# Memory attention of a decoder layer: TensorE's instructions in the order of emission

## The chip, the cores and the metric

The kernel runs on one core of a Trainium2 chip. The time is that of the device for one execution of the whole program, in microseconds (us), as the median over runs. The core has five engines that run side by side, each with its own queue of instructions: TensorE (PE, with its weight loads as PEld), VectorE (DVE), ScalarE (ACT), GpSimd (POOL) and SyncE (SP), which here issues the DMA transfers.

## The reference

The program computes one decoder layer for 1024 tokens with d_model 1024: a half-step SwiGLU, then three branches from one projection (A: chunked spatial gating, B: causal latent attention, C: cross-attention into 256 memory tokens), their gated merge, an output projection and a second half-step SwiGLU. All inputs are float32. What this case touches is branch C, and the product of branch A with its weights that runs in between:

```python
def memory_attention(q_m, mem, mem_norm, w_kv, q_norm, k_norm):
    q = rmsnorm(q_m.reshape(B, S, MEM_HEADS, MEM_HEAD_DIM), q_norm)      # 4 heads of 128
    kv = rmsnorm(mem, mem_norm) @ w_kv
    k = rmsnorm(kv[..., :MEM_WIDTH].reshape(B, M, MEM_HEADS, MEM_HEAD_DIM), k_norm)
    v = kv[..., MEM_WIDTH:].reshape(B, M, MEM_HEADS, MEM_HEAD_DIM)       # M = 256
    s = jnp.einsum('bshd,bmhd->bhsm', q, k).astype(jnp.float32) * (MEM_HEAD_DIM ** -0.5)
    p = jax.nn.softmax(s, axis=-1)
    return jnp.einsum('bhsm,bmhd->bshd', p.astype(v.dtype), v).reshape(B, S, MEM_WIDTH)
...
merged = (gates[:, :, 0] * (y_a @ w_branch_a[l])      # the product that fills in
          + gates[:, :, 1] * (y_b @ w_branch_b[l])
          + gates[:, :, 2] * (y_c @ w_branch_c[l]))
```

## The kernel before

**Number format.** To keep float32 accuracy on TensorE, every operand is split in a rounded part and a rest (hi and lo, type fp32r). `split` does it: ScalarE copies to hi (L139), VectorE subtracts to lo (L142). A product is then three matmuls, `mm3`: hi by hi (L158), hi by lo (L159), lo by hi (L160).

**The stage.** `mem_attention` (L857) comes after the spatial gating and ahead of the causal attention. It works on eight tiles of 128 queries, numbered (i, k) with i = 0..3 and k = 0..1; two tiles make a pair i. It is a list of calls of small functions, written out by hand, with these letters:

- `S` (`scores`, L862): four heads, each one `mm3` of 256 columns, into one PSUM tile `mm` (two buffers): 12 matmuls. Then VectorE takes the extreme of each row (L874) and scales it (L878), ScalarE takes four exponentials (L882), VectorE the reciprocals of the sums (L886), GpSimd multiplies (L887).
- `T` (`turn`, L890): the eight transposes of a tile's probabilities (L934), in two calls of `to_feature4`, each four transposes into one PSUM tile `bank` and one `split`. "The eight turns of each tile" are these. `T` raises the priority of what it emits.
- `V` (`value`, L901): the product of a pair's probabilities with the values: 24 matmuls of 256 columns into two `bank` tiles, each split at once.
- `F` (a step of `branches`, L527): 12 matmuls of 512 columns of branch A's product into one `bank` tile, which VectorE multiplies with the gate (L1117) and SyncE stores. There are 16 such steps, called blocks here. `A` is such a step too, with an order for its casts on ScalarE.
- `Q` (`mem_queries`, L850): eight DMA loads (L855), of 256 KB each, of one half (512 tokens) of the queries: hi and lo of four heads. The tiles of heads 0 and 1 are called `h`, those of heads 2 and 3 `v_hi` and `v_lo`, after the buffers that they live in.
- `R`: a rotation on GpSimd that belongs to the next stage.

There are four `bank` buffers in all, for blocks, turns and values together.

**What sets the order.** The framework has a scheduler: before the program is built, it lays the instructions of each engine in one fixed order, by their priority (which falls in the order of emission, and which `T` raises) and by when, in its own model of time, their operands are there. The order on an engine at run time is that fixed order; an engine waits at an instruction whose operands are late, and nothing behind it passes. Parts of the program stand in a region (`manual_schedule`) in which named engines keep the order of emission instead. `mem_attention` stands in none before the change, so that the matmuls of blocks, scores, turns and values are mixed by the scheduler. SyncE's queue, too, is laid out by the scheduler.

Of the kernel before, what the change touches and what calls it, by code (L numbers as in the profile page):

```python
# [18 lines left out]
S = 1024  # L19
DT = D // P  # L20
NT = S // P
F = 2816
# [27 lines left out]
class Kernel:  # L50
# [806 lines left out]
    def mem_attention(self, qt, rooms, kt, vv, filler, after, aside):  # L857

        nc = self.nc
        r, nr = self.mq_r, self.mq_nr  # L860
        st, scaled = {}, []

        def scores(i, k):
            t = 2 * i + k
            sc = self.mm().rearrange("p a (b m) -> p (a b) m", b=2)
            for hh in range(MH):
                last = self.last
                first = self.mm3(
                    sc[:, hh], tuple(x[:, t * P:(t + 1) * P] for x in qt[hh]), tuple(x[:, hh] for x in kt),
                    True, True)  # L870
                if i == hh == 0:
                    self.after(first, last)
            mx = self.stat("m_mx", MH)
            m = nc.vector.tensor_reduce(mx, sc, axis=AXX, op=ALU.min)  # L874
            if scaled:
                self.after(m, scaled.pop())
            with self.tc.high_priority(offset=600):
                scaled.append(nc.vector.tensor_tensor(mx, mx, r[:, t], op=ALU.mult))  # L878
            pr = rooms[t % len(rooms)]
            sm = self.stat("m_sm", MH)  # L880
            for hh in range(MH):
                nc.scalar.activation(  # L882
                    pr[:, hh], sc[:, hh], ACT.Exp, bias=mx[:, hh:hh + 1], scale=nr[:, t, hh:hh + 1],
                    accum_out=sm[:, hh:hh + 1])
            rs = self.stat("m_rs", MH)
            nc.vector.reciprocal(rs, sm)  # L886
            nc.gpsimd.tensor_tensor(pr, pr, rs.unsqueeze(2).to_broadcast([P, MH, ML]), op=ALU.mult)  # L887
            st[i, k] = pr

        def turn(i, k):  # L890
            if k == 0:
                st[i] = [tuple(self.wide(n).rearrange("p (h q) -> p h q", h=MH) for n in ("whi", "wlo")) for _ in range(2)]
            pr = st.pop((i, k))
            for m in range(2):
                with self.tc.high_priority(offset=600):
                    self.to_feature4(
                        tuple(t[:, :, k * P:(k + 1) * P] for t in st[i][m]),
                        [pr[:, hh, m * P:(m + 1) * P] for hh in range(MH)])

        def value(i):  # L900
            pt = st.pop(i)  # L901
            for pair in range(MH // 2):
                o = self.bank().rearrange("p (b q) -> p b q", b=2)
                for hh in (2 * pair, 2 * pair + 1):
                    for m in range(2):
                        s = tuple(t[:, m, hh * MD:(hh + 1) * MD] for t in vv)
                        self.mm3(o[:, hh % 2], s, tuple(t[:, hh] for t in pt[m]), m == 0, m == 1)
                for hh in (2 * pair, 2 * pair + 1):
                    self.split(*(t[:, 2 * i * P:2 * (i + 1) * P] for t in yt[hh]), o[:, hh % 2])

        S, T, V = scores, turn, value
        R = lambda: aside(behind=self.last)
        F = lambda: next(filler, None)
        Q = lambda half: self.mem_queries(qt, half, self.sig_mark)

        def A():
            self.hold = after
            F()
            self.hold = None

        yt = [self.split_pair(self.h4) for _ in range(MH)]
        for f, *x in (
                (A,), (A,), (Q, 0), (S, 0, 0), (A,), (S, 0, 1), (F,), (F,), (Q, 1), (T, 0, 0), (S, 1, 0), (F,), (T, 0, 1), (S, 1, 1),
                (F,), (F,), (V, 0), (T, 1, 0), (S, 2, 0), (F,), (T, 1, 1), (S, 2, 1), (F,), (V, 1), (F,), (T, 2, 0),
                (S, 3, 0), (F,), (T, 2, 1), (S, 3, 1), (R,), (F,), (V, 2), (F,), (T, 3, 0), (F,), (T, 3, 1), (F,), (V, 3)):
            f(*x)
        for _ in filler:
            pass
        return yt
# [1402 lines left out]
```

## Time and profile before

| what | value |
|---|---|
| time, median of 3 runs | 2164.04 us (2162.85 to 2164.99) |
| the profiled execution | 2163.03 us, of which 2161.3 us are the span of the profile |
| granted TensorE clock, mean | 0.999 of full speed |
| busy share of the span: PE, DVE, ACT, POOL | 100%, 73%, 42%, 12% |
| the stage from its first block to its last value matmul | 1134.46 to 1209.18 us of the span |

In the rows of a timeline the first number is the start of a group of like instructions in us from the start of the span, the second how long the group took, and the text in brackets the idle time of the engine ahead of it with what ended it. Matmuls are pipelined: one ends after the next has begun, so that the pace of TensorE is read from one start to the next, not from the length of one.

### The profile page before, as it was taken

The page shows a single profiled execution, that of the slowest core. Times are in us where ns is not written, and L with a number is a line of the kernel's source. Part 1 is how long each engine was busy: PE and PEld are TensorE (multiplying, and loading weights), DVE is VectorE, ACT ScalarE, POOL GpSimd, SP SyncE. Part 2 cuts the span into 40 slices and gives each one's busy share as a digit, 9 for nine tenths or more (in the row PEclk, how much of TensorE's full clock was granted, in tenths as well). Part 3 has the DMA queues.
Part 4 walks back from the last instruction along what each step waited for, and adds up shares of the span by engine and source line. Part 5 has one row for each costly group of instructions (what it writes and reads, how often), then busy time and mean ns, then how long its engine had stood idle before and what let it go on. Part 6 is the DMA issues. An engine that isn't in the chain of part 4 may idle for free.

```text
span 2161.3 us, 27448 instructions
## 1 busy us (share of the span) xinstructions
PE 2151.9 (100%) x10112; PEld 1797.8 (83%) x10112; DVE 1572.1 (73%) x2371; ACT 910.3 (42%) x1486; POOL 255.0 (12%) x256
## 2 busy tenths in 40 slices
PE   9999999999999999999999999999999999999999
PEld 6888888888887888888988889988888888888887
DVE  7966666679889657655786679886876666657884
ACT  6433333243455434433555378833433223224332
POOL 0011111100000000000123311240011212110000
PEclk9999999999999999999999999999999999999999
DMA  4264555385332445641587832293133332347443
GB/s 148 92 220 159 190 180 175 119 318 193 118 124 94 147 164 180 223 149 61 212 283 259 314 105 69 75 348 104 40 127 103 110 97 100 103 144 288 169 129 104
DMA packets 137175, 342.56 MB, mean 158 GB/s; under 512 B 21713, under 2 KB 30033, under 8 KB 137041
## 3 DMA queue, kind: packets, MB, share of 16 engines
q1 hardware_dynamic: 136896, 340.81, 45.9%
q8 instruction: 79, 1.29, 0.2%
q14 instruction: 56, 0.45, 0.1%
q10 hardware_dynamic: 144, 0.00, 0.0%
HBM read 230.90 MB, written 109.86 MB: 158 GB/s over the span
## 4 chain that ended last, share of the span: by engine, by line
PE 91%; DVE 6%; ACT 1%; DMA 1%; issue 1%; SPq 0%; POOL 0%; ACTq 0%; DVEq 0%; POOLq 0%
PE one L158 15%; PE one L159 15%; PE one L160 15%; PE bank L158 13%; PE bank L159 13%; PE bank L160 13%; PE mm L158 1%; PE mm L159 1%; PE mm L160 1%; PE bank L1019 1%; PE one L1967 1%; DVE w L147 1%; DVE wlo L147 1%; DVE pr L997 1%; DVE wlo L142 1%
## 5 line engine op out<-in xcount | busy, mean ns | idle before, releaser
L146 ACT CAST whi<-x 128x1024 fp32r<-128x1024 f32 x202 | 192.3, 955 | 414.4 <-DVE x L1443 170.4
L147 DVE TENSOR_TENSOR wlo<-x,whi 128x1024 fp32r<-128x1024 f32 x202 | 241.2, 1195 | 58.9 <-ACT whi L146 19.6
L1471 DVE TENSOR_TENSOR t<-t,one 128x512 f32<-128x512 f32 x188 | 128.9, 686 | 190.8 <-PE one L160 190.7
L158 PE MATMUL bank<-h,whi 128*128 128x512 f32 x636 | 247.9, 390 | 0.0
L160 PE MATMUL bank<-h,wlo 128*128 128x512 f32 x636 | 247.5, 389 | 0.0
L159 PE MATMUL bank<-h,whi 128*128 128x512 f32 x636 | 247.5, 389 | 0.0
L158 PE MATMUL one<-h,whi 128*128 128x512 f32 x508 | 199.0, 392 | 0.0
L159 PE MATMUL one<-h,whi 128*128 128x512 f32 x508 | 198.4, 390 | 0.0
L160 PE MATMUL one<-h,wlo 128*128 128x512 f32 x508 | 198.3, 390 | 0.0
L158 PE MATMUL one<-w,whi 128*128 128x512 f32 x432 | 168.5, 390 | 0.0
L159 PE MATMUL one<-w,whi 128*128 128x512 f32 x432 | 168.1, 389 | 0.0
L160 PE MATMUL one<-w,wlo 128*128 128x512 f32 x432 | 168.1, 389 | 0.0
L142 DVE TENSOR_TENSOR wlo<-w,whi 128x1024 fp32r<-128x1024 f32 (+2 forms) x112 | 114.4, 1036 | 67.3 <-ACT whi L139 67.1
L139 ACT CAST whi<-w 128x1024 fp32r<-128x1024 f32 (+2 forms) x112 | 98.8, 901 | 149.8 <-PE one L159 55.6
L2067 POOL TENSOR_TENSOR raw<-raw 128x512 f32<-128x512 f32 x38 | 57.0, 1499 | 794.8 <-DVE raw L1908 684.8
L160 PEld LDWEIGHTS bank<-h,wlo 128*128 128x128 f32 x636 | 119.4, 188 | 24.9
L159 PEld LDWEIGHTS bank<-h,whi 128*128 128x128 f32 x636 | 119.4, 188 | 24.6
L158 PEld LDWEIGHTS bank<-h,whi 128*128 128x128 f32 x636 | 119.4, 188 | 24.4
L158 PE MATMUL bank<-whi 128*128 128x512 f32 x352 | 136.9, 389 | 0.0
L159 PE MATMUL bank<-wlo,whi 128*128 128x512 f32 x352 | 136.9, 389 | 0.0
L160 PE MATMUL bank<-whi,wlo 128*128 128x512 f32 x352 | 136.9, 389 | 0.0
L160 PEld LDWEIGHTS one<-h,wlo 128*128 128x128 f32 x508 | 95.8, 189 | 20.1
(406 smaller groups left out, 4892.2 us busy)
## 6 DMA issues: line engine op xcount, KB each, us to landing
x<-in_ffn_w_gu_dram SPq DMA_DIRECT2D x78, 512.0 KB, 5.1
w<-tdt SPq DMA_DIRECT2D x40, 512.0 KB, 4.2
gate<-raw SPq DMA_DIRECT2D x33, 512.0 KB, 3.0
tdb<-raw SPq DMA_DIRECT2D x64, 256.0 KB, 2.1
h<-in_ffn_w_down_dram SPq DMA_DIRECT2D x64, 256.0 KB, 6.0
w<-tdb SPq DMA_DIRECT2D x30, 512.0 KB, 5.1
tdt<-w SPq DMA_DIRECT2D x48, 256.0 KB, 2.4
x<-in_w_gate_dram SPq DMA_DIRECT2D x22, 512.0 KB, 5.9
```

The costliest lines, as they stand in the source:

```text
L139: i = self.nc.scalar.copy(hi, src)
L142: return (eng or self.nc.vector).tensor_tensor(lo, src, hi.bitcast(F32), op=ALU.subtract)
L146: self.nc.scalar.copy(hi, src)
L147: return lambda: self.nc.vector.tensor_tensor(lo, src, hi.bitcast(F32), op=ALU.subtract)
L158: i = mmul(out, s[0], m[0], start=first, stop=False, **kw)
L159: mmul(out, s[0], m[1], start=False, stop=False, **kw)
L160: self.last = mmul(out, s[1], m[0], start=False, stop=last, **kw)
L997: nc.vector.tensor_tensor_reduce(out=pr[:, :m], in0=sc[:, :m], in1=self.mask[:, m0:m0 + m], scale=1.0, scalar=-NEG, op0=ALU.add, op1=ALU.m ...
L1019: nc.tensor.transpose(b[:, at:at + P], prs[t][:, kk * P:(kk + 1) * P], self.ident)
L1471: return self.nc.vector.tensor_tensor(out, x, y, op=ALU.add)
L1967: k.last = nc.tensor.matmul(b, w, norm.x(half, c), start=c == 0, stop=c == DT - 1)
L2067: sub = lambda d, x, y: (eng or nc.gpsimd).tensor_tensor(d, x, y, op=ALU.subtract)
```

## The change

The list of calls is put into a region in which TensorE keeps the order of emission. The list itself, the arithmetic, the buffers and the other engines' instructions are as before; the order of the other engines stays with the scheduler.

```diff
         yt = [self.split_pair(self.h4) for _ in range(MH)]
-        for f, *x in (
-                (A,), (A,), (Q, 0), (S, 0, 0), (A,), (S, 0, 1), (F,), (F,), (Q, 1), (T, 0, 0), (S, 1, 0), (F,), (T, 0, 1), (S, 1, 1),
-                (F,), (F,), (V, 0), (T, 1, 0), (S, 2, 0), (F,), (T, 1, 1), (S, 2, 1), (F,), (V, 1), (F,), (T, 2, 0),
-                (S, 3, 0), (F,), (T, 2, 1), (S, 3, 1), (R,), (F,), (V, 2), (F,), (T, 3, 0), (F,), (T, 3, 1), (F,), (V, 3)):
-            f(*x)
+        with self.tc.manual_schedule(engines={mybir.EngineType.PE}):
+            for f, *x in (
+                    (A,), (A,), (Q, 0), (S, 0, 0), (A,), (S, 0, 1), (F,), (F,), (Q, 1), (T, 0, 0), (S, 1, 0), (F,), (T, 0, 1), (S, 1, 1),
+                    (F,), (F,), (V, 0), (T, 1, 0), (S, 2, 0), (F,), (T, 1, 1), (S, 2, 1), (F,), (V, 1), (F,), (T, 2, 0),
+                    (S, 3, 0), (F,), (T, 2, 1), (S, 3, 1), (R,), (F,), (V, 2), (F,), (T, 3, 0), (F,), (T, 3, 1), (F,), (V, 3)):
+                f(*x)
```

## Rows read from the trace of the kernel before

**Rows 1.** The page: the chain that ended last, by engine.
```profile
PE 91%; DVE 6%; ACT 1%; DMA 1%; issue 1%; SPq 0%; POOL 0%; ACTq 0%; DVEq 0%; POOLq 0%
```

**Rows 2.** Busy time of each engine in the stage, clock, DMA share, GB/s.
```profile
1134.46:1209.18 74.72, 74.30 (x451) 65.77 (x450) 52.09 (x94) 42.00 (x115) 21.41 (x16) 1.00 0.71 246
```

**Rows 3.** The timeline of TensorE at its only pause in the stage.
```profile
1152.38 0.28 PE L160 MATMUL mm<-h,v_lo 128*128 128x256 f32 x1
1153.08 0.39 PE L158 MATMUL mm<-h,h 128*128 128x256 f32 x1 [0.42 <-ACT v_hi L882]
```

**Rows 4.** TensorE's groups by line in the stage: count, busy us, mean ns.
```profile
L158 PE MATMUL bank<-x,whi 128*128 128x512 f32 x64 | 25.8, 404 | 0.0
...
L159 PE MATMUL bank<-wlo,h 128*128 128x256 f32 x32 | 9.0, 285 | 0.0
...
L158 PE MATMUL mm<-h,h 128*128 128x256 f32 x16 | 4.7, 294 | 0.4 <-ACT v_hi L882 0.4
L934 PE MATMUL bank<-ident,v_hi 128*128 128x128 f32 x32 | 4.6, 272 | 0.0
```

**Rows 5.** The timeline of TensorE: starts in runs of blocks and of scores.
```profile
1135.00 0.40 PE L160 MATMUL bank<-x,wlo 128*128 128x512 f32 x1
...
1140.00 0.39 PE L158 MATMUL bank<-x,whi 128*128 128x512 f32 x1
...
1151.07 0.28 PE L158 MATMUL mm<-h,h 128*128 128x256 f32 x1
```

**Rows 6.** The timeline of TensorE: eight turns together, and four of eight.
```profile
1154.38 1.04 PE L934 MATMUL bank<-ident,v_hi 128*128 128x128 f32 x8
1155.17 0.48 PE L158 MATMUL bank<-x,whi 128*128 128x512 f32 x1
...
1172.61 0.60 PE L934 MATMUL bank<-ident,v_lo 128*128 128x128 f32 x4
1172.96 0.48 PE L158 MATMUL bank<-x,whi 128*128 128x512 f32 x1
1173.27 0.40 PE L159 MATMUL bank<-x,whi 128*128 128x512 f32 x1
```

**Rows 7.** The timeline of TensorE: the first matmul of the first scores.
```profile
1143.63 0.28 PE L158 MATMUL mm<-h,h 128*128 128x256 f32 x1
```

**Rows 8.** The timeline of SyncE: a load for a later stage, first and last query loads.
```profile
1135.30 0.38 SPq L565 DMA_DIRECT2D x<-gate  x1
1135.72 0.43 SPq L855 DMA_DIRECT2D h<-mq  x1
...
1138.35 0.32 SPq L855 DMA_DIRECT2D h<-mq  x1
```

**Rows 9.** Time to landing of the `h` loads issued at 1135.72 and 1138.35.
```profile
h<-mq SPq DMA_DIRECT2D x1, 256.0 KB, 6.6
...
h<-mq SPq DMA_DIRECT2D x1, 256.0 KB, 5.9
```

**Rows 10.** The timelines of VectorE and GpSimd: from the first scores to their turns.
```profile
1147.01 1.22 DVE L874 TENSOR_REDUCE m_mx<-mm 128x4 f32<-128x1024 f32 x1 [1.28 <-PE mm L160]
...
1151.27 1.90 POOL L887 TENSOR_TENSOR v_hi<-v_hi,m_rs 128x1024 f32<-128x1024 f32 x1 [42.16 <-DMA v_hi<-mq]
```

**Rows 11.** The one fall of the clock: busy time by windows (PEclk third from the end).
```profile
36.00:39.30 3.30, 3.30 (x29) 3.17 (x28) 2.67 (x7) 1.52 (x2) 0.00 (x0) 1.00 0.00 0
39.40:42.80 3.40, 3.40 (x10) 2.60 (x9) 2.56 (x8) 0.00 (x0) 0.00 (x0) 0.50 0.00 0
```

**Rows 12.** The timeline of TensorE in that fall.
```profile
35.89 2.73 PE L394 MATMUL bank<-ones,t 128*128 128x1 f32 x24
...
40.01 0.63 PE L160 MATMUL one<-h,wlo 128*128 128x512 f32 x1
40.43 0.63 PE L158 MATMUL one<-h,whi 128*128 128x512 f32 x1
```

**Rows 13.** Busy time of each engine in the causal attention that follows.
```profile
1240.00:1400.00 160.00, 158.58 (x1110) 145.11 (x1110) 137.96 (x301) 130.06 (x290) 29.88 (x78) 1.00 0.25 79
```

## The prediction, made before the changed kernel ran

> **What bounds the kernel now.** I read the chain that ended last first: it is TensorE for 91% [rows 1], so a microsecond that TensorE loses or saves in this stage is, to a first look, a microsecond of the program. Then the busy times of the stage: TensorE is busy for 74.30 of 74.72 us, at the full clock, while VectorE has 52.09 and GpSimd 21.41 [rows 2]. The timeline shows one pause of TensorE, 0.42 us ahead of a score matmul that waited for exponentials to free its PSUM buffer [rows 3]. From start to start that is 0.70 us where 0.12 is usual, so 0.58 us are lost there. The reader is to see that the scheduler's mixture is nearly free of waits: what a new order can win in this stage is small, and what it can lose is not bounded in the same way.
>
> How small, I work out from the pace. A block has 12 matmuls of 512 columns; from 1135.00 to 1140.00 there are 22 starts, 0.2273 us each [rows 5], so a block takes 2.73 us. Scores have 12 matmuls of 256 columns: eleven steps from 1151.07 to 1152.38 [rows 3, 5] are 0.119 each, so 1.43 us a tile, and by the same pace 2.87 us for the 24 of a value step. Eight turns together take 0.79 us from their first start to the next matmul [rows 6], and the matmul behind a group of turns takes 0.31 instead of 0.23 to hand over to the next (1172.96 to 1173.27) [rows 6], so 0.87 for a tile's turns. The counts are 3 x 64 block matmuls (16 blocks), 96 of the values (4 steps), 6 x 16 of the scores (8 tiles) and 64 turns (8 tiles) [rows 4], where the other hi and lo forms of each kind have like rows. The sum is 16 x 2.73 + 8 x 1.43 + 4 x 2.87 + 8 x 0.87 = 43.7 + 11.4 + 11.5 + 7.0 = 73.6 us. The stage took 74.7 [rows 2]. So 1.1 us is all that a perfect order could win in it.
>
> **Keeping eight turns together.** This is what the change says that it does. In the trace six of the eight tiles have their turns in two groups of four, two in one group. Four turns take 0.35 us and the matmul behind them 0.08 more [rows 6], so a tile in two groups costs 2 x 0.43 = 0.86, against 0.87 in one. The six changes of kind that go away are paid back by the slower pace within a group of eight (0.099 a turn against 0.088). I cost this edit at 0; from the two sums it can't be more than 0.1 us either way in all.
>
> **What the forced order moves.** The step that matters is the first score tile. In the list, two blocks stand ahead of it. The blocks begin at 1134.46 as before, since nothing ahead of the list is touched, and two of them end at 1134.46 + 5.46 = 1139.9. There S(0,0) now has to start. In the trace it starts at 1143.63 [rows 7], with 9.17 / 0.2273 = 40 block matmuls ahead of it, not 24. The reason stands in SyncE's queue. The loads of heads 0 and 1 are issued from 1135.72 to 1138.35 [rows 8] and land 6.6 and 5.9 us later [rows 9]: the first at 1142.3, the fourth at 1144.25. The scheduler had put 16 block matmuls into that hole; the forced order forbids it, and nothing else can fill it: what was emitted ahead of the list is done, and what comes after it needs this stage's results.
>
> So S(0,0) is paced by the landings. Its first matmul waits until 1142.3. The last of its seven remaining matmuls after the fourth landing comes at 1144.25 + 0.1 (a hand-over, estimated from TensorE's last score to the reduce, which follows closely) + 7 x 0.119 = 1145.2. Without the wait it would end at 1139.9 + 1.43 = 1141.35. The stall is 3.85 us.
>
> Are the landings the same after the change? Up to S(0,0) both orders are the same on TensorE, so the scheduler sees the same buffers come free at the same time, and the query loads already stand as early in SyncE's queue as their buffers allow. I take them as unchanged. The bounds: the 512 KB load for a later stage that goes ahead of them [rows 8] could slip behind, which by the spacing of the 256 KB loads (four landings in 2 us, so 1.3 us for 512 KB) would take 1.3 us off the stall; or one more such load could go ahead, which would add 1.3.
>
> **What follows behind the stall.** From 1145.2 on there remain 14 blocks, 7 score tiles, 8 tiles of turns, 4 value steps: 38.2 + 10.0 + 7.0 + 11.5 = 66.7 us, so the last value matmul ends at 1211.9, against 1209.18 [rows 2]. That is +2.75 us: 3.85 of stall less the 1.1 that the order of before lost. This needs that no other step of the list waits. The longest chain is from scores to turns: the reduce of S(0,0) starts at 1147.01 and GpSimd ends at 1151.27 + 1.90 = 1153.17 [rows 10], 6.2 us. In the list there stand a block, S(0,1) and two blocks between S(0,0) and T(0,0), 3 x 2.73 + 1.43 = 9.6 us; behind the other scores at least 10. So the turns don't wait, with 3 us to spare, and the PSUM buffers of the scores are free before they are asked for again, which also removes the pause of [rows 3]. Value steps stand a score tile and a block (4.2 us) behind their last turns, the first one two blocks and a score tile, the last one a block alone, as in the trace. Only the splits lie between, about 2 us by the trace; that is covered unless a reduce of 1.22 us [rows 10] stands in front on VectorE. Each such wait would cost up to 1.2 us; I take none.
>
> The second half of the queries is asked for in the list behind the fifth block and used by S(2,0), with 3 tiles of turns, 2 of scores, 3 blocks and a value step between, 2.6 + 2.9 + 8.2 + 2.9 = 16.6 us. Eight loads at the spacing of the first half (0.66 us) and with its 6.6 us to landing [rows 9] need 6.6 + 7 x 0.66 = 11.2 us; I cost them at nothing. The stage behind this one is bound by TensorE as well: in the causal attention TensorE is busy for 158.58 of 160 us, VectorE for 138 [rows 13]. It begins 2.75 us later and has no slack of TensorE to give it back, so the whole amount reaches the end.
>
> **The clock.** At 39.4 us the granted clock falls from 1.0 to 0.5, that is from 2.4 to 1.2 GHz, for a stretch of 3.4 us [rows 11]. What TensorE did before were 24 one-column matmuls and a few wide ones [rows 11, 12], without an idle gap. In the fall a wide matmul takes 0.42 us from start to start [rows 12] instead of 0.23, so such a stretch costs 3.4 x (1 - 0.23/0.42) = 1.55 us. The stall here leaves TensorE idle for 2.4 us and then thinly used for two more, which is a similar sight. The Trainium skill ("TensorE: Matmul & The Clock Gate", section "HAM oscillation — how this bites in real kernels") says that a wait for a DMA between bursts of matmuls can put the array back to its slow clock, so that the next burst starts cold. By that rule the sum would be 1.55 us higher or more. No row here shows a wait of this length in mid-kernel, so whether it bites is open; the fall at 39.4 us agrees that the clock can fall late in a program, though no idle wait stood ahead of that one.
>
> **The sum.** Turns 0, stall +3.85, waits of before that go away -1.1: +2.75 us. Against the profiled execution, 2163.03 us (1.7 outside its span), that gives 2165.8. That execution lies 1.0 below the median of the runs shown, and I forecast the median: 2164.04 + 2.75 = 2166.8. A measurement can tell about 0.2%, 4.3 us, from no change; so this is a small loss that counts as the same.
>
> **The rivals.**
>
> - *Slower, by the clock.* The stall puts the array to 1.2 GHz for one stretch like that of [rows 11], +1.55 us, so 2168.4, just at the bound of 0.2%; for two of them +3.1, so 2169.9, and beyond it. For it: the fall at 39.4 us. Against it: in all the later stages the trace shows full clock, though with no such stall. It decides from the second stretch on.
> - *Slower, by more waits.* Value steps wait behind VectorE, up to 1.2 us at each of four, up to +4.8, so up to 2171.6; it passes the bound at the second wait. Against it: VectorE is busy for only 52 of 74.7 us [rows 2]. The same size covers a less lucky order that the scheduler may find for the following attention, where VectorE is close behind TensorE [rows 13].
> - *The change doesn't stall.* SyncE's order shifts in favour of the queries, or the wait is filled with something that I don't see. Then up to 1.1 us are won: 2162.9. Against it: SyncE's order depends on buffers that come free no earlier.
> - *Faster beyond 0.2%.* It would need 4.3 us, four times what the stage loses. Only a luckier order in later stages could give it.
>
> **How the numbers follow.** The forecast (stall, nothing else) has 0.50, with 2165.3 to 2168.2 for the bounds of the query landings; the clock 0.18; more waits 0.14; no stall 0.14; faster 0.04. Half of the clock's share, most of the further waits' and a little of the forecast's tail lie above 2168.4: slower 0.24. Faster 0.04, the rest 0.72. For 8 in 10 the range goes from the case without a stall, 2162.9, to two stretches at half clock, or three or four further waits, 2171.
>
> **What would show it.** Right: TensorE idle from 1139.9 until about 1142.3 and in two more short gaps, released by DMA; S(0,0) ending near 1145; turns in eight groups of eight with no wait ahead; the last value matmul near 1211.9; the later stages moved by the same 2.75 us. Wrong: queries that land well before or after 1142 to 1144; a PEclk of 0.5 behind the gap; waits ahead of turns or values; a different length of the stretch behind the stage.

## The result, and the profile after

| | before | changed | ratio, 95% interval |
|---|---|---|---|
| median of the runs | 2163.93 us (14 runs, 2161.28 to 2165.35) | 2168.29 us (14 runs, 2165.70 to 2171.79) | 1.0023 [1.0016, 1.0030] |
| profiled execution | 2163.03 us | 2166.94 us | |
| its span | 2161.3 us | 2165.2 us | |
| the stage | 74.72 us [rows 2] | 79.28 us | |

The loss of 4.36 us lies inside the range and on the side that was forecast, but it is 1.6 us larger than the forecast's own loss of 2.75 us. It ends just past the 0.2% (4.3 us) that was called the same, and its interval holds both sides of that bound. It is the time of the rival "slower, by the clock" (2168.4), not that of the forecast (2166.8).

The stage first. The windows of the changed kernel give, for the whole stage, for the wait in it, for the stretch behind the wait and for the attention that follows (length; busy time of TensorE, its weight loads, VectorE, ScalarE and GpSimd; granted clock, DMA share, GB/s):

```profile
1134.56:1213.84 79.28, 76.49 (x451) 67.14 (x450) 52.21 (x92) 40.82 (x114) 21.84 (x16) 0.98 0.66 228
1140.20:1144.60 4.40, 1.61 (x7) 0.97 (x7) 4.15 (x7) 0.12 (x1) 0.00 (x0) 1.00 1.03 385
1144.65:1148.00 3.35, 3.35 (x12) 2.91 (x12) 1.39 (x2) 0.32 (x1) 0.00 (x0) 0.50 0.89 273
1240.00:1400.00 160.00, 159.10 (x1114) 145.76 (x1113) 136.76 (x298) 127.94 (x286) 30.29 (x79) 1.00 0.26 83
```

Against [rows 2] TensorE does the same 451 instructions in 4.56 us more. In the second row it is busy for only 1.61 of 4.40 us, and in the third it is busy all the time, at half the clock. The other engines' sums are within 1.2 us of those before. The attention behind the stage is as full as in [rows 13].

The timeline of TensorE in the changed kernel, from the last matmul of the two first blocks into the block behind the first scores (start, duration, line, tile; in brackets the idle time ahead and what ended it):

```profile
1139.88 0.39 PE L160 MATMUL bank<-x,wlo 128*128 128x512 f32 x1
1142.50 0.36 PE L158 MATMUL mm<-h,h 128*128 128x256 f32 x1 [2.23 <-DMA h<-mq]
...
1143.75 0.39 PE L158 MATMUL mm<-h,h 128*128 128x256 f32 x1 [0.26 <-DMA h<-mq]
...
1144.41 0.42 PE L160 MATMUL mm<-h,h 128*128 128x256 f32 x1 [0.16 <-DMA h<-mq]
1144.63 0.41 PE L158 MATMUL mm<-h,v_hi 128*128 128x256 f32 x1
...
1145.91 0.63 PE L158 MATMUL bank<-x,whi 128*128 128x512 f32 x1
1146.34 0.63 PE L159 MATMUL bank<-x,whi 128*128 128x512 f32 x1
...
1148.04 0.40 PE L160 MATMUL bank<-x,wlo 128*128 128x512 f32 x1
1148.28 0.40 PE L158 MATMUL bank<-x,whi 128*128 128x512 f32 x1
```

The first score matmul starts at 1142.50 instead of 1143.63 [rows 7], and has 24 block matmuls ahead of it instead of 40. The three waits are on the query loads. SyncE issues these loads in the order of [rows 8], and the first and the fourth land 6.8 and 6.3 us after their issue, against 6.6 and 5.9 [rows 9]:

```profile
1135.11 0.39 SPq L565 DMA_DIRECT2D x<-gate  x1
1135.54 2.81 SPq L855 DMA_DIRECT2D h<-mq  x4
...
h<-mq SPq DMA_DIRECT2D x1, 256.0 KB, 6.8
...
h<-mq SPq DMA_DIRECT2D x1, 256.0 KB, 6.3
```

From the timeline the 4.56 us can be split. The two blocks end at 1139.88 + 0.23 = 1140.11, the first scores at 1145.91: 5.80 us for a tile of 1.43, so 4.37 too many. The last six of its matmuls take (1145.91 - 1144.63) / 6 = 0.213 us instead of 0.119: 0.57 of the 4.37 are the slow clock, the other 3.80 are waiting. The next five starts, from 1145.91 to 1148.04, take 2.13 us where 5 x 0.2273 = 1.14 is usual, 0.99 more. From 1144.63 to 1148.04 is a stretch of 3.41 us at half clock, which costs 0.57 + 0.99 = 1.56 us. What is left, 4.56 - 3.80 - 1.56 = -0.80, is what the new order wins back: from 1145.91 to 1213.84 there are 67.93 us, 66.94 without the 0.99 of the clock, and no turn and no value step waits. The turns are eight groups of eight; this is one of them in the same timeline, 0.79 us from its start to the next matmul, as in [rows 6]:

```profile
1156.57 1.03 PE L935 MATMUL bank<-ident,v_hi 128*128 128x128 f32 x8
1157.36 0.36 PE L158 MATMUL mm<-h,h 128*128 128x256 f32 x1
```

Behind the stage the changed kernel loses nothing more: from the last value matmul to the end of the span it takes 2165.2 - 1213.8 = 951.4 us, before 2161.3 - 1209.2 = 952.1.

### The profile page after: what moved, and what is told of

Its sections match the earlier page's. It is cut to its first block, busy times and chain, and to the rows that moved or that the text cites. A ratio compares the mean times of both kernels' runs of the same rounds, so it can differ in the third digit from the quotient of the medians.

```text
span 2165.2 us, 27446 instructions
## 1 busy us (share of the span) xinstructions
PE 2153.6 (99%) x10112; PEld 1798.9 (83%) x10112; DVE 1572.8 (73%) x2371; ACT 909.6 (42%) x1486; POOL 254.6 (12%) x256
## 4 chain that ended last, share of the span: by engine, by line
PE 91%; DVE 6%; ACT 1%; DMA 1%; issue 1%; SPq 0%; POOL 0%; ACTq 0%; DVEq 0%; POOLq 0%
PE one L158 15%; PE one L159 15%; PE one L160 15%; PE bank L158 13%; PE bank L159 12%; PE bank L160 12%; PE mm L160 1%; PE mm L158 1%; PE mm L159 1%; PE bank L1020 1%; DVE wlo L147 1%; DVE pr L998 1%; PE bank L1968 1%; PE one L1968 1%; DVE wlo L142 1%
```

## The experiments

The theory after this: the loss is the wait for the query loads, forced by the place of the first scores in the list, and a fall of the clock that this wait brings on. Its rivals: the loss comes from the forced order as such (other waits, or the turns kept together), or the fall of the clock stands where it does by chance. Each experiment is built on the changed kernel. Ratios are to the kernel before, measured beside it.

**The changed kernel, twice again.**

> The changed kernel itself, once more, for a second profile and more times beside the other kernels of this job. Theory (the wait lets the clock fall behind it): a gap of 2 to 3 us ahead of the first scores, released by the query loads, PEclk 0.5 for 3.4 us close behind it, 2167 to 2169. Rival (the fall in the first profile was chance): the same gap with PEclk 1.0 behind it.

> The changed kernel itself beside the filled one, on the same chip. Theory: a fall of the clock close behind the wait for the third time, 2167 to 2169.

They gave 2167.64 us (1.0022 [1.0013, 1.0031]) and 2168.66 us (1.0025 [1.0017, 1.0034]), with stages of 79.3 and 79.6 us. The windows behind the wait, of the first and then of the second:

```profile
1145.30:1148.60 3.30, 3.30 (x12) 2.91 (x12) 1.39 (x2) 0.23 (x1) 0.00 (x0) 0.50 0.84 268
```
```profile
1145.70:1149.00 3.30, 3.30 (x12) 2.72 (x11) 1.39 (x2) 0.88 (x3) 0.00 (x0) 0.50 1.00 367
```

So the fall stands close behind the wait in three of three profiles of the changed kernel; it isn't an accident of one execution.

**The first scores later: two more blocks ahead of them, two fewer further down.**

```diff
-(A,), (A,), (Q, 0), (S, 0, 0), (A,), (S, 0, 1), (F,), (F,), (Q, 1), ...
-(F,), (F,), (V, 0), (T, 1, 0), ... (V, 1), (F,), (T, 2, 0),
+(A,), (A,), (Q, 0), (A,), (F,), (S, 0, 0), (F,), (S, 0, 1), (F,), (F,), (Q, 1), ...
+(F,), (V, 0), (T, 1, 0), ... (V, 1), (T, 2, 0),
```

> The changed kernel with two more blocks ahead of the first score tile and two fewer further on, all still in the order of emission. Theory (the loss is the wait for the queries and the clock that falls behind it): the first scores come at about 1145.4 us, after the last query of heads 0 and 1 has landed, TensorE has no gap over 0.3 us in the stage, the clock stays at 1.0, the stage lasts 73.6 to 74.3 us, and the time is that of the kernel before or up to 1.1 us less: 2162.8 to 2164. Rival (the forced order costs something all along the stage, in turns and values): 2165 or more, with waits ahead of turns or values.

Measured 2164.02 us, 0.9999 [0.9990, 1.0008]: the whole loss is gone, with the order forced as before and the turns together. The stage in its windows, and the first score matmul in its timeline, with no wait ahead of it:

```profile
1133.06:1207.27 74.21, 74.21 (x451) 65.85 (x450) 53.81 (x94) 41.52 (x115) 22.18 (x16) 1.00 0.69 244
...
1144.04 0.28 PE L158 MATMUL mm<-h,h 128*128 128x256 f32 x1
```

TensorE is never idle in this stage, and the clock is full. 74.21 against 74.72 us is the half microsecond that was still to be won in it; over the program it can't be told from nothing. That the order is forced costs nothing that can be told, then; that the first scores stand ahead of their queries does. One reservation: the eleven times fall into two groups, four near 2160.8 us at a mean clock of 1.000 and seven near 2164.7 us at 0.999, and the profile is of the first group. The ratio is over all of them, but what the 3.9 us between the groups are, no profile shows.

**The first scores earlier: one block ahead of them instead of two.**

```diff
-(A,), (A,), (Q, 0), (S, 0, 0), (A,), (S, 0, 1),
+(A,), (Q, 0), (S, 0, 0), (A,), (A,), (S, 0, 1),
```

> The changed kernel with one block less ahead of the first scores and one more behind. Theory (the first scores are paced by the landing of the queries, not by TensorE): they end where they end in the changed kernel, or up to 0.7 us earlier since one gate load less stands ahead of the query loads; the gap is 2 to 2.7 us longer, the clock falls behind it, and the time is 2 to 2.7 us more than that of the changed kernel: 2170 to 2171.5. Rival (the queries are loaded when TensorE comes to need them): the wait stays as it is, 2168.

Measured 2170.41 us, 1.0037 [1.0024, 1.0050], 2.8 us above the changed kernel measured beside it. The first score matmul in the timeline, the time to landing of the first query load of heads 0 and 1, and the windows of the stage and of the slow clock:

```profile
1142.48 0.55 PE L158 MATMUL mm<-h,h 128*128 128x256 f32 x1 [6.43 <-DMA h<-mq]
...
h<-mq SPq DMA_DIRECT2D x1, 256.0 KB, 8.2
...
1133.07:1217.17 84.10, 77.61 (x451) 68.23 (x450) 53.13 (x94) 41.62 (x115) 21.84 (x16) 0.94 0.63 217
1139.00:1149.20 10.20, 6.66 (x20) 5.50 (x21) 4.64 (x8) 2.58 (x7) 0.00 (x0) 0.50 1.02 368
```

The first scores still start when the queries land, but this takes longer here: the first load needs 8.2 us to landing instead of 6.8, and the first score matmul starts 9.41 us into the stage instead of 7.94. So of the 4.20 us by which the wait is longer, 2.73 are the block that no longer stands ahead of it and 1.47 the later landing. The longer wait has a longer stretch at half clock: 10.2 us, which begins inside the wait. The stage is 4.8 us longer than the changed kernel's. The times show only 2.8 of it: this profile lacks the fall at 39 us [rows 11], and its stage begins 2.2 us earlier in the span than in the changed kernel's profile taken beside it. That 2.8 comes so near to the 2 to 2.7 expected is in part luck.

**The first six entries of the list outside the forced region.**

```diff
+for f, *x in steps[:6]:
+    f(*x)
 with self.tc.manual_schedule(engines={mybir.EngineType.PE}):
-    for f, *x in (...):
+    for f, *x in steps[6:]:
         f(*x)
```

> The region begins behind the second score tile: the first three blocks and two score tiles are left to the scheduler, all from there on keeps the order of emission, so that the turns of each tile stay together. Theory: the scheduler puts blocks into the wait as in the kernel before, nothing else costs, and the stage lasts 73.6 to 74.7 us, the time is 2163 to 2164.3. Rival (the order of turns and values costs): 2165 or more. A third outcome would be that later blocks can't be drawn ahead, since they are in the region, so that only one block fills the wait: a gap of about 1 us stays, 2164.5 to 2165.5.

Measured 2164.33 us, 1.0007 [0.9998, 1.0016]. The stage, and its two longest waits of TensorE (us in total, times, the longest):

```profile
1134.76:1210.92 76.16, 74.37 (x451) 65.78 (x450) 53.21 (x93) 41.31 (x115) 21.84 (x16) 1.00 0.69 236
...
PE bank L938 <- POOL v_hi L887: 1.5, 1, 1.5
PE mm L158 <- DMA h<-mq: 0.3, 1, 0.3
```

The scheduler fills the hole of the queries with blocks again, as before the change, and the clock stays full. But these blocks are then missing between the scores and their turns, in the part that is forced: the first turns now wait 1.5 us for GpSimd, the end of the chain of 6.2 us from scores to turns [rows 10] that the prediction had found covered. Neither the theory nor its rival had this wait. A wait of this length, at the full clock ahead and behind, brought no fall.

**Each tile's turns in two groups of four, in the order with late scores.**

```diff
-def turn(i, k):
+def turn(i, k, m):
     ...
-(T, 0, 0), (S, 1, 0), (F,), (T, 0, 1), (S, 1, 1), ...
+(T, 0, 0, 0), (S, 1, 0), (T, 0, 0, 1), (F,), (T, 0, 1, 0), (S, 1, 1), (T, 0, 1, 1), ...
```

> The kernel with two more blocks ahead of the first scores, with each tile's eight turns in two groups of four, a score tile, a block or a value step between them. Theory (keeping the turns together is worth nothing): the stage is within 0.4 us of that with the turns together, the time within 1 us of it. Rival (each change between turns and matmuls costs something that the pace within a group doesn't give back): eight more changes at 0.08 us or more, the stage longer by 0.7 us or more.

Measured 2163.72 us, 1.0004 [0.9995, 1.0013], the same as with the turns together. Its stage:

```profile
1135.08:1210.44 75.36, 74.44 (x451) 65.68 (x450) 55.83 (x95) 41.59 (x117) 22.38 (x16) 1.00 0.72 252
```

TensorE is busy for 74.44 us against 74.21 with the turns together, so keeping them together is worth 0.2 us of its time, by one profile of each. The other 0.9 of the 1.15 us by which this stage is longer are two waits late in the stage: 0.7 us in the last value step, for a split on VectorE, and 0.2 us for GpSimd ahead of the turns of tile (3, 0), which stand ahead of a value step in this list and behind it in the other.

**The scores of heads 2 and 3 first in the first tile.** Their queries are loaded ahead of those of heads 0 and 1.

```diff
-for hh in range(MH):
+for hh in ((2, 3, 0, 1) if t == 0 else range(MH)):
```

> The changed kernel, in which the first score tile takes heads 2 and 3 first, whose queries land some 2 us ahead of those of heads 0 and 1. Theory: six matmuls (0.7 us) move from behind the wait to ahead of it, the stage is 0.7 us shorter, the clock still falls: 2167 to 2168. If the clock does not fall, 2166. Rival (the wait is for something else than the loads of heads 0 and 1): no change, 2168.3.

Measured 2167.37 us, 1.0022 [1.0013, 1.0031], against 2167.64 for the changed kernel beside it. In the timeline six matmuls now stand in the hole and the wait is 1.60 us long; the fall comes nevertheless. The second row is the matmul that needs the last query; the last two are the windows of the slow clock and of the stage:

```profile
1141.94 0.39 PE L158 MATMUL mm<-h,h 128*128 128x256 f32 x1 [1.60 <-DMA h<-mq]
...
1144.02 0.58 PE L160 MATMUL mm<-h,h 128*128 128x256 f32 x1 [0.23 <-DMA h<-mq]
...
1143.90:1147.20 3.30, 3.18 (x8) 2.60 (x9) 1.39 (x2) 1.02 (x4) 0.00 (x0) 0.50 0.87 307
...
1133.59:1212.65 79.06, 76.69 (x451) 67.24 (x450) 51.87 (x93) 41.12 (x114) 21.84 (x16) 0.98 0.67 229
```

With the six matmuls gone, the part of the stage behind the start of that matmul is 0.80 us shorter. But the last query lands later: that matmul starts 10.43 us into the stage, against 1144.41 - 1134.56 = 9.85 in the changed kernel. So the stage is 79.06 us long, only 0.22 less. For the program no gain can be told.

**The wait filled with matmuls that nobody uses.** To part the clock from the wait, I put matmuls of 512 columns into the hole. They write a part of the PSUM tile that the scores overwrite, so they change no result; the work is added. Three amounts: 8 ahead of head 0; 10 there and 1 ahead of head 1; and 15, which also fill the short waits.

```diff
+if t == 0 and hh < 2:
+    for _ in range((10, 1)[hh]):
+        nc.tensor.matmul(sc[:, 2:4], kt[0][:, 0, :P], kt[0][:, :2], start=True, stop=True)
 first = self.mm3(...)
```

> The changed kernel with eight extra matmuls of 512 columns (1.8 us) ahead of the first scores, none between their heads; the engines' orders are those of the changed kernel but for a few places in this stage. The first such experiment, with eleven, kept the clock up in this stage, but a small transfer of the next stage landed 3 us later there and took the gain. Theory (clock): the first scores still wait for the last query, PEclk stays 1.0 behind the wait, and the stage is 1.0 to 1.6 us shorter than that of the changed kernel in this job, counted from the end of the first scores; 2166 to 2167.5 if the next stage is not disturbed. Rival (filling the wait does nothing to the clock): PEclk 0.5 behind the wait, same length as the changed kernel.

> The changed kernel, with eleven extra matmuls of 512 columns in the wait (ten ahead of head 0 of the first scores, one ahead of head 1), which write to a part of that tile that is overwritten later. They add 2.5 us of work that ends before the queries land. Theory (two costs: 2.75 us of waiting, and 1.6 us of a clock that falls because TensorE did little): the wait stays as long, the clock does not fall behind it, the time is 2166 to 2167, and the runs scatter less than those of the changed kernel. Rival (the clock fell for another reason, or the extra 1.6 us isn't the clock): 2168 or more, PEclk 0.5 behind the wait as before.

> The changed kernel with fifteen extra matmuls of 512 columns in the wait: ten ahead of head 0 of the first scores, then two, two and one in the three short waits between the query landings, so that TensorE is busy all through. The engines' orders are those of the changed kernel but for a few places in this stage. Theory (waiting costs 2.75 us, the clock 1.6 or a little more): no fall of the clock in the stage, which lasts 77.4 to 78 us in the profile against 79.2; the mean granted clock over the runs comes close to that of the kernel before, and the time is 2165.5 to 2167. Rival (the clock falls in other places instead, so that filling the wait wins nothing): the mean granted clock as in the changed kernel, about 0.9984, 2167.5 or more. A late transfer of the next stage, as with eleven fillers, would show as waits of TensorE near 1300 us and is counted apart.

In the order 8, 11, 15 they gave 2168.43 us (1.0025 [1.0015, 1.0035]), 2171.30 us (1.0039 [1.0026, 1.0051]) and 2170.08 us (1.0034 [1.0022, 1.0047]). In time all three missed. In the stage they did what the theory asks. The stage of the kernel with 15, the matmul that needs the last query, and the stretch that holds the wait and what follows:

```profile
1134.78:1212.23 77.45, 77.45 (x466) 68.53 (x464) 52.92 (x92) 40.91 (x113) 21.86 (x16) 1.00 0.67 231
...
1144.37 0.39 PE L160 MATMUL mm<-h,h 128*128 128x256 f32 x1
...
1142.00:1147.50 5.50, 5.50 (x31) 4.61 (x30) 3.95 (x7) 0.45 (x1) 0.00 (x0) 1.00 0.95 311
```

The same matmul and the stage with 8 extra matmuls, and then with 11:

```profile
1144.61 0.39 PE L160 MATMUL mm<-h,h 128*128 128x256 f32 x1
...
1134.32:1212.47 78.15, 76.77 (x459) 67.38 (x458) 52.08 (x92) 41.03 (x114) 21.83 (x16) 1.00 0.67 233
```
```profile
1145.84 0.39 PE L160 MATMUL mm<-h,h 128*128 128x256 f32 x1 [0.18 <-DMA h<-mq]
...
1134.83:1213.69 78.86, 77.45 (x463) 67.87 (x462) 52.42 (x93) 41.34 (x114) 21.85 (x16) 1.00 0.66 231
```

The clock stays full in this stage in all three profiles. The stages are 77.45, 78.15 and 78.86 us long, against 79.3, 79.3 and 79.6 in the three profiles of the changed kernel, but the queries don't land at the same point of each. The matmul that needs the last query starts 9.59, 10.29 and 11.01 us into these stages, and 9.85, 9.86 and 10.21 us into the changed kernel's. Counted from its start, what is left of the stage takes 67.86, 67.86 and 67.85 us with the extra matmuls, and 69.43 us in each of the three profiles without. So the slow clock costs the stage 1.57 us, as worked out above (1.56).

The program is no shorter, because the next stage takes the gain back and more: with 15 it takes 956.1 us from the last value matmul to the end, with 11 956.6, with 8 952.6, in the changed kernel 951.4. The traces of the first two tell where most of it goes. Three rows of three timelines (GpSimd, VectorE, TensorE) of the kernel with 15:

```profile
1295.45 1.29 POOL L1071 TENSOR_TENSOR ysum<-ysum,t 128x512 f32<-128x512 f32 x1 [10.51 <-DMA t<-invd]
...
1297.43 0.69 DVE L142 TENSOR_TENSOR x<-ysum,x 128x512 fp32r<-128x512 f32 x1 [2.76 <-ACT x L139]
...
1299.88 0.52 PE L1023 MATMUL bank<-ident,pr 128*128 128x128 f32 x3 [1.90 <-DVE wlo L142]
```

and the first two in the changed kernel:

```profile
1293.66 1.29 POOL L1068 TENSOR_TENSOR ysum<-ysum,t 128x512 f32<-128x512 f32 x1 [7.12 <-DMA t<-invd]
...
1296.18 0.68 DVE L142 TENSOR_TENSOR x<-ysum,x 128x512 fp32r<-128x512 f32 x1
```

A small load `t<-invd` (128 KB, the reciprocal sums of the attention, read back from DRAM) lands late; GpSimd multiplies by it 83.2 us behind the last value matmul instead of 79.8, the split on VectorE stands in its order until then and holds up all that is behind it there, and TensorE waits 1.90 us (3.0 us in all three waits at this line). With 11 the same row shows 1.81 us (2.7 us in all), and a second stretch at half clock right behind it:

```profile
1301.23 0.52 PE L1024 MATMUL bank<-ident,pr 128*128 128x128 f32 x3 [1.81 <-DVE wlo L142]
...
1302.20:1305.40 3.20, 3.20 (x17) 3.18 (x17) 2.19 (x4) 2.29 (x5) 0.00 (x0) 0.50 0.00 0
```

With 15 there is no such stretch behind the longer of the two waits:

```profile
1301.00:1304.00 3.00, 2.70 (x24) 2.46 (x22) 2.43 (x5) 2.67 (x6) 0.00 (x0) 1.00 0.00 0
```

The load is the second of a pair; it lands 6.3 us after its issue in the changed kernel (7.0 and 4.6 in its other two profiles, 6.9 with 8 extra matmuls, 7.8 in the kernel before), but 9.8 with 11 and 9.5 with 15. In the stretch around these loads the engines take their instructions in the changed kernel's order. Why the load is late there stays open. So the price of the clock is shown in the stage, by six profiles; at the level of the whole program these three kernels don't show it.

## Why the prediction was right and where it was wrong

**Right: the wait and its place.** Predicted 3.85 us of stall, paced by landings at 1142.3 and 1144.25; measured 3.80, with landings at 1135.54 + 6.8 = 1142.3 and, from 1138.03, 6.3 later, 1144.3. SyncE's order did not shift. That this wait is what the change costs is shown by the runs that move the first scores: two blocks later it is gone and with it the loss, one block earlier it is longer by that block and by the later landing there.

**Right: the turns.** Costed at 0; they go into eight groups at the pace of [rows 6], and splitting them in the same forced order moves TensorE's busy time by 0.2 us (0.1 was the most that the prediction's sums allowed) and the program by nothing that can be measured.

**Right, a little high: what the order wins back.** 66.7 us were predicted from the end of the first scores to the last value matmul; without the slow clock it was 66.9, and the two blocks ahead took 5.55 instead of 5.46. So 0.8 us came back, not 1.1. The sum of 73.6 us for a perfect order was too low: with late scores TensorE is never idle and the stage takes 74.21. No turn or value step waited, and the following attention gave back 0.7 us where I expected none: a wait of 0.50 us for VectorE in it was gone.

**Wrong: the sum left the clock out.** The step that failed is the one headed "The clock". It had the sight (idle 2.4 us, then thinly used for two more), the price (1.55 us for one stretch) and the time that would follow (2168.4), and gave that 0.18, on the ground that the later stages show no fall. But the later stages of before hold no such wait, as the prediction says itself, so they were no evidence against it. The measured stretch is 3.41 us long and costs 1.56; with it the sum of the prediction is 2168.4, and the median was 2168.29. That they meet so closely is in part luck: the stage lost 4.56 us where that sum has 4.3, and the stages behind it gave back 0.7 in the profile. In all five profiles in which the first scores wait unfilled for their queries (the changed kernel three times, heads 2 and 3 first, early scores) the clock falls there, and in none of the seven others (before, late scores, region later, split turns, three fills) does it fall in this stage. The Trainium skill ("TensorE: Matmul & The Clock Gate", section "HAM oscillation — how this bites in real kernels") says that a wait for a DMA between bursts of matmuls can put the array back to its slow clock; these traces agree, for a wait of 2.23 us followed by six thinly spaced matmuls. Not each wait does it: 1.5 us ahead of turns (region later) and 1.90 us behind the stage (15 extra matmuls) brought no fall, while 1.81 us (11 extra) did.

The times say the same as far as they reach. A stretch of 3.41 us at half clock is 3.41 / 2 / 2165 = 0.0008 of a run's mean granted clock, and in the twelve profiles the mean reads 1.000 with no stretch, 0.999 with one, and 0.998 with two or with the long one of early scores. Of the 68 runs of before measured beside the experiments, 36 read 1.000 and 32 read 0.999. Of the 36 runs of the changed kernel none reads 1.000: 14 read 0.999 (2167.18 us on average), 19 read 0.998 (2168.70) and 3 read 0.997. So by this reading each run of the changed kernel had at least one stretch, as a fall behind the wait asks. In its three profiles the second stretch is the one at 39 us [rows 11], which comes and goes by itself. Why 22 of 36 runs have a second one or more, where 32 of 68 of before have one at all, stays open; it may be chance.

**The chances.** The bound between same and slower (4.3 us) lay between the forecast (2.76) and the clock's case (4.4), so 0.72 for same hung on the clock above all. With the fall taken as the likelier case, same and slower would have stood at about equal chances. The bounds of the forecast hold a small slip as well: 1.3 us to either side of 2166.8 is 2165.5 to 2168.1, not 2165.3 to 2168.2.

## What to carry to other kernels

Before an engine is made to keep a written order, look for the transfer that its first step needs: where it lands, where the engine will arrive, and which independent work the scheduler had put between; two blocks moved ahead of the first scores took the whole loss away here. Price a wait on TensorE with what the clock takes behind it, 3.8 us of waiting and 1.6 us of slow clock in this case, and don't take a trace without such a wait as evidence that the clock will stay up. Work moved ahead into one hole is missing between later steps: with the region begun later the hole of the queries was filled, and the first turns waited 1.5 us for GpSimd.

## What the runs showed of the hardware that was not expected

- The wait doesn't have to be empty: with six matmuls in the hole and 1.60 us of idle time the clock still fell for a stretch of the same size. And the length of the wait doesn't decide alone: 1.5 us ahead of turns (region later) and 1.90 us in the next stage (15 extra matmuls), both with dense work on both sides, brought no fall, while 1.81 us at the latter place (11 extra) did. What tells them apart isn't shown.
- A wait of 6.43 us had 10.2 us at half clock, three times the stretch of the 2.23 us wait.
- The fall at 39.4 us [rows 11] isn't there in each execution: in four of the twelve profiles (late scores, early scores, 8 extra matmuls, heads 2 and 3 first) this stretch stands at 1.00, though the code there is the same.
- The landing of one 128 KB load, with the same instructions around it, came 4.6 to 9.8 us after its issue over the profiles of the changed kernel and of the three fills. The landings at 9.8 and 9.5 us went with waits of TensorE of 1.81 and 1.90 us, the others with none of this size.
